# Decay rows of a head stored in one piece in DRAM: one 4096-byte run per partition in the broadcast read

## The chip, the cores and the metric

The kernel runs on one core of one Trainium2 chip. The metric is the device time of one execution in microseconds (us). A core has TensorE (PE), VectorE (DVE), ScalarE (ACT), GpSimd (POOL) and SyncE (SP), which issues nearly all transfers here, and 16 DMA engines that move the data. The engines run apart from one another and meet at semaphores.

## The reference, cut to what matters

One encoder layer in float32, 512 tokens, width 1024. The part that the change touches is a gated delta rule with 8 heads, in both directions of the sequence, in chunks (64 in the reference; the kernel uses 128). Its decay comes from a cumulative sum `gc` over each chunk:

```python
g = -exp(a_log) * softplus(a + dt_bias)          # one number per token, direction and head
gc = cumsum(g, axis=-1)                          # within a chunk
diff = gc[..., :, None] - gc[..., None, :]
decay = where(incl, exp(where(incl, diff, 0.0)), 0.0)
lmat = where(strict, einsum('nbhcd,nbhsd->nbhcs', kb, k) * decay, 0.0)
attn = einsum('nbhcd,nbhsd->nbhcs', q, k) * decay
q_dec = q * exp(gc)[..., None]
```

Around it stand the projections of x by w_in (9216 columns and 32 more), a short convolution branch, two layer norms and a feed-forward part of width 4096.

## The kernel before

Every product of full size is made in three passes over a high and a low part (`xh`, `xl` of the activations, `wh`, `wl` of the weights). A weight block of 128x1024 comes in by one transfer on SP's queue (`raw_in`, 512 KB, line 110, three buffers), ACT makes `wh` from it (line 124), DVE makes `wl` (line 120), and PE runs 24 products of 128x512 (lines 158 to 160, `ps_in`). A load can be issued when DVE has finished with the buffer.

The delta rule is woven into these projections. The code is written as generators, and a loop over slots h = 0..8 sets the order on PE, DVE, ACT and POOL by hand: tables such as `BEGIN` and `MID` say after which step of the projections the next piece of a generator is taken. SP's queue is left to a scheduler. From slot 1 to slot 5 every slot has the same six weight blocks (three of the next head's q, k and v and three of the rest). In each there runs the second half of `gdn_local` of head h (`mid`), the first half of `gdn_local` of head h+1 (`new`) and the scan of head h-1 (`far`).

What the change touches: the cumulative sums of all heads lie in `gc` as 128 tokens by 64 rows (2 directions, 4 chunks, 8 heads). They are transposed to `gct` (64 rows of 128 tokens) and written to `gcd` in DRAM (line 337). For each head, `gdn_local` reads the head's eight rows back to all 128 partitions as `grow` (128 x 8 x 128, 512 KB, line 446, three buffers). DVE makes `dec` from it (line 451), ACT takes the exponential of both (lines 454 and 455), POOL multiplies `grow` with q (line 480), and PE reads the result in the scan (line 660).

What else the prediction speaks of: in the second half of `gdn_local` an inverse of small triangular blocks is made. POOL makes `X` (lines 536 to 550), it goes through DRAM (`xo`, line 555) to `U` (line 559), and PE then runs bursts of very small products: 64 of 32x32 at line 571 (`px`) and 64 at line 580 (`py`), then 32 and 16 at each of the lines 600 and 612 (`pxa`, `pya`, `pxb`, `pyb`). On SP's queue `U`, one `raw_in`, the `grow` of a later head (heads 3 to 7 in the slots 1 to 5) and further `raw_in` follow one another.

Of the kernel before, what the change touches and what calls it, by code (L numbers as in the profile page):

```python
# [8 lines left out]
F32 = mybir.dt.float32  # L9
# [6 lines left out]
P = 128  # L16
# [3 lines left out]
NH = 8  # L20
NCH = 4
# [40 lines left out]
def kernel(  # L62
# [25 lines left out]
    nc = tc.nc  # L88
# [10 lines left out]
    dram = ctx.enter_context(tc.tile_pool(name="dram", bufs=1, space=bass.MemoryType.DRAM))  # L99
# [113 lines left out]
    for d in range(2):  # L213
        t = cons.tile([P, P], F32, name=f"tri{d}")
# [64 lines left out]
    def sm(name, shape=(P, NCH, 16)):  # L279
        return cons.tile(list(shape), F32, name=name)  # L280
# [52 lines left out]
    nc.tensor.transpose(pgt[:64, :P], gcf, ident)  # L333
    gct = sm("gct", (64, P))
    nc.vector.tensor_copy(out=gct, in_=pgt[:64, :P])
    gcd = dram.tile([64, P], F32, name="gcd")
    nc.sync.dma_start(out=gcd, in_=gct)
    urgent.close()
    gcd_v = gcd.rearrange("(d c h) t -> h (d c) t", d=2, c=NCH)


    eye = cons.tile([P, 8, 16], F32, name="eye")
    for g in range(2):
        for t in range(2):
            nc.sync.dma_start(out=eye.rearrange("(b g) (s t) j -> g t b s j", g=2, t=2)[g, t],
                              in_=diag[2 * t + g, 0:4, 0:16].partition_broadcast(P // 2))
# [96 lines left out]
    def gdn_local(h):  # L443

        grow = gdn.tile([P, 2 * NCH, P], F32, tag="grow", name=f"grow{h}", bufs=3)
        nc.sync.dma_start(out=grow, in_=gcd_v[h].partition_broadcast(P))
        yield
        dec = gnear.tile([P, 2 * NCH, P], F32, tag="dec", name=f"dec{h}", bufs=1)
        for c in range(NCH):
# [31 lines left out]
            out=qd, in0=qd,  # L481
            in1=qk[:, 1, :].rearrange("p (c t) -> p c t", t=P).unsqueeze(1).broadcast_to([P, 2, NCH, P]), op=ALU.mult)
        na_ = gdn.tile([P, 2, 2, NCH, P], F32, tag="na", name=f"na{h}", bufs=2)
        for g2 in range(2):
            yield
            pg = ps("g", f"pg{h}_{g2}")
            for cc in range(2):
                c = 2 * g2 + cc
# [25 lines left out]
        for g in range(2):  # L514
            nc.sync.dma_start(out=Nb.rearrange("(b g) i j -> g b (i j)", g=2)[g],
                              in_=xd.rearrange("x a i j -> (x a) (i j)"))
# [21 lines left out]
        t = tmp[:, :7 * 16].rearrange("p (m j) -> p m j", j=16)  # L538
# [3 lines left out]
        for k in range(0, 16, 2):  # L542
# [3 lines left out]
            t = tmp[:, :r * 2 * n].rearrange("p (i m j) -> p i m j", m=2, j=n)  # L546
# [5 lines left out]
        for s_ in range(2):  # L552
            for g in range(2):
                o = slice(16 * s_, 16 * s_ + 16)
                nc.sync.dma_start(out=xo[:, :, o, o].rearrange("x a (r g) j -> g (x a) r j", g=2)[g],
                                  in_=X.rearrange("(b s g) r j -> s g b r j", s=2, g=2)[s_, g])
# [190 lines left out]
    def local(h):  # L747
        state[h] = yield from gdn_local(h)
# [67 lines left out]
    for c in range(8):  # L816
# [11 lines left out]
        t = slab.tile([P, NT], F32, tag="C", name=f"yb{c}", bufs=8)  # L828
        act(out=t, in_=pyb, func=AF.Copy)
        yb.append(t)  # L830
    for c in range(8):
        pgb = proj(w_in[B_GB + c], xh, xl, f"in{B_GB + c}")
        t = slab.tile([P, NT], F32, tag="zt", name=f"sgb{c}", bufs=2)
# [9 lines left out]
    for c in range(8):  # L843
        pga = proj(w_in[B_GA + c], xh, xl, f"in{B_GA + c}")
        t = slab.tile([P, NT], F32, tag="D", name=f"sga{c}", bufs=8)
# [222 lines left out]
```

## Time and profile before

| what | value |
|---|---|
| three runs | 1066.55, 1070.11 and 1071.96 us, median 1070.11 us |
| the profiled execution | 1075.07 us, its span 1073.4 us (from the first to the last instruction) |
| mean granted TensorE clock in it | 0.984 |
| PE busy | 1031.4 us, 96% of the span |
| DVE, ACT, POOL busy | 529.7, 452.6 and 286.6 us |
| moved by DMA | 101.79 MB in 64269 packets |

The profiled execution is 4.96 us above the median. Products on PE are pipelined and their ends are modelled, so busy time is not a measure of work; an idle gap on PE is. The granted clock is 1.00 at 2.4 GHz and 0.50 at 1.2 GHz.

### The profile page before, as it was taken

What the parts mean: (1) busy time and instruction counts of PE and PEld (TensorE: products, weight loads), DVE (VectorE), ACT (ScalarE), POOL (GpSimd) and SP (SyncE); (2) the same over time, 40 slices, a digit from 0 to 9 for tenths busy, and PEclk for the clock granted to TensorE, in tenths of its full rate; (3) what the DMA queues carried; (4) which work ended last, traced back from release to release, by engine and by line L of the source; (5) the groups of instructions that cost most, each with busy time, mean ns of one, the idle gap of its engine ahead of it and who ended that gap; (6) DMA issues with size and microseconds to landing.
All of it is one profiled execution on the core that took longest, in us unless ns stands there. A gap on an engine that the chain in (4) does not pass through costs nothing.

```text
span 1073.4 us, 16601 instructions
## 1 busy us (share of the span) xinstructions
PE 1031.4 (96%) x6611; PEld 854.3 (80%) x6611; DVE 529.7 (49%) x923; ACT 452.6 (42%) x820; POOL 286.6 (27%) x527
## 2 busy tenths in 40 slices
PE   8897989997999999999999999989999999999996
PEld 5676878886878887888888888879888888888885
DVE  6574657665766767352322255581222233333346
ACT  5562546664656575463424233222333343222231
POOL 1061524351535253430131011063222220000005
PEclk9998989998999999999999999999999999999998
DMA  5412242323242513222336324322333343333312
GB/s 197 138 47 88 67 105 67 88 67 87 67 87 67 107 49 92 69 79 79 99 99 233 96 85 138 115 78 63 96 98 98 98 133 102 98 98 94 102 41 79
DMA packets 64269, 101.79 MB, mean 95 GB/s; under 512 B 30720, under 2 KB 40640, under 8 KB 64192
## 3 DMA queue, kind: packets, MB, share of 16 engines
q1 hardware_dynamic: 63760, 100.07, 32.5%
q8 instruction: 52, 0.85, 0.3%
q10 hardware_dynamic: 432, 0.66, 0.2%
q14 instruction: 25, 0.20, 0.1%
HBM read 97.27 MB, written 3.44 MB: 94 GB/s over the span
## 4 chain that ended last, share of the span: by engine, by line
PE 83%; DVE 6%; DMA 3%; POOL 3%; issue 2%; ACT 1%; SPq 1%; POOLq 0%; DVEq 0%; ACTq 0%
PE accd L899 16%; PE ps_in L158 11%; PE ps_in L160 10%; PE ps_in L159 10%; PE ps_up L158 5%; PE ps_up L159 5%; PE ps_up L160 5%; PE acco L899 3%; POOL X L550 2%; PE psup L946 1%; PE ps_osc L158 1%; PE ps_osc L160 1%; PE ps_ogd L158 1%; PE ps_ogd L160 1%; PE ps_osc L159 1%
## 5 line engine op out<-in xcount | busy, mean ns | idle before, releaser
L158 PE MATMUL ps_in<-xh,wh_in 128*128 128x512 f32 x576 | 241.2, 419 | 1.2 <-ACT wh_in L124 1.1
L160 PE MATMUL ps_in<-xh,wl_in 128*128 128x512 f32 x576 | 228.6, 397 | 1.8 <-DVE wl_in L120 1.8
L159 PE MATMUL ps_in<-xl,wh_in 128*128 128x512 f32 x576 | 227.9, 396 | 0.0
L120 DVE TENSOR_TENSOR wl_in<-raw_in,wh_in 128x1024 fp32r<-128x1024 f32 x70 | 95.1, 1358 | 87.1 <-ACT wh_in L124 82.2
L160 PEld LDWEIGHTS ps_in<-xh,wl_in 128*128 128x128 f32 x576 | 109.8, 191 | 27.6 <-DVE wl_in L120 3.0
L158 PEld LDWEIGHTS ps_in<-xh,wh_in 128*128 128x128 f32 x576 | 110.5, 192 | 22.7 <-ACT wh_in L124 2.0
L159 PEld LDWEIGHTS ps_in<-xl,wh_in 128*128 128x128 f32 x576 | 110.8, 192 | 18.3
L124 ACT ACTIVATE wh_in<-raw_in 128x1024 fp32r<-128x1024 f32 x70 | 73.9, 1056 | 71.0 <-PE ps_in L159 52.9
L899 PE MATMUL accd<-wh_down,hh 128*128 128x512 f32 x256 | 99.5, 389 | 0.0
L899 PE MATMUL accd<-wl_down,hh 128*128 128x512 f32 x256 | 99.4, 389 | 0.0
L899 PE MATMUL accd<-wh_down,hl 128*128 128x512 f32 x256 | 99.4, 389 | 0.0
L120 DVE TENSOR_TENSOR wl_up<-raw_up,wh_up 128x1024 fp32r<-128x1024 f32 x30 | 36.8, 1225 | 121.5 <-ACT wh_up L124 121.5
L158 PE MATMUL ps_up<-x1h,wh_up 128*128 128x512 f32 x224 | 87.1, 389 | 0.0
L159 PE MATMUL ps_up<-x1l,wh_up 128*128 128x512 f32 x224 | 87.1, 389 | 0.0
L160 PE MATMUL ps_up<-x1h,wl_up 128*128 128x512 f32 x224 | 87.1, 389 | 0.0
L953 POOL TENSOR_TENSOR hf<-r 128x512 f32<-128x512 f32 x32 | 46.3, 1447 | 118.5 <-ACT r L951 118.5
L124 ACT ACTIVATE wh_up<-raw_up 128x1024 fp32r<-128x1024 f32 x30 | 31.8, 1060 | 106.2 <-PE ps_up L159 98.6
L106 DVE TENSOR_TENSOR wl_down<-raw_down,wh_down 128x1024 fp32r<-128x1024 f32 x32 | 40.1, 1254 | 50.3 <-ACT wh_down L105 48.8
L899 PEld LDWEIGHTS accd<-wh_down,hl 128*128 128x128 f32 x256 | 48.1, 188 | 10.1
L899 PEld LDWEIGHTS accd<-wl_down,hh 128*128 128x128 f32 x256 | 48.1, 188 | 10.0
L899 PEld LDWEIGHTS accd<-wh_down,hh 128*128 128x128 f32 x256 | 48.0, 188 | 10.1 <-ACT wh_down L105 0.4
L105 ACT ACTIVATE wh_down<-raw_down 128x1024 fp32r<-128x1024 f32 x32 | 33.7, 1053 | 51.0 <-PE accd L899 50.3
(268 smaller groups left out, 1853.1 us busy)
## 6 DMA issues: line engine op xcount, KB each, us to landing
raw_in<-in_w_in SPq DMA_DIRECT2D x70, 512.0 KB, 3.7
raw_up<-in_w_up SPq DMA_DIRECT2D x32, 512.0 KB, 3.6
raw_down<-in_w_down SPq DMA_DIRECT2D x32, 512.0 KB, 3.6
grow<-gcd SPq DMA_DIRECT2D x8, 512.0 KB, 10.0
raw_osc<-in_w_o_sc SPq DMA_DIRECT2D x8, 512.0 KB, 3.6
raw_ogd<-in_w_o_gdn SPq DMA_DIRECT2D x8, 512.0 KB, 3.6
raw_out<-in_w_out SPq DMA_DIRECT2D x8, 512.0 KB, 3.7
xr<-in_xT SPq DMA_DIRECT2D x8, 256.0 KB, 5.1
```

What stands on the lines that cost most here:

```text
L105: act(out=hi, in_=src, func=AF.Copy)
L106: (lo_eng or nc.vector).tensor_tensor(out=lo, in0=src, in1=hi.bitcast(F32), op=ALU.subtract)
L120: (nc.gpsimd if pool else nc.vector).tensor_tensor(out=wl, in0=raw, in1=wh.bitcast(F32), op=ALU.subtract)
L124: act(out=wh, in_=raw, func=AF.Copy)
L158: nc.tensor.matmul(acc, wh[:, c], mh[k], start=(k == 0), stop=False)
L159: nc.tensor.matmul(acc, wh[:, c], ml[k], start=False, stop=False)
L160: nc.tensor.matmul(acc, wl[:, c], mh[k], start=False, stop=(k == KT - 1))
L550: sub(out=X[:, 0:r, k + 1:16], in0=X[:, 0:r, k + 1:16], in1=t[:, :, m], op=ALU.add)
L899: nc.tensor.matmul(acc[:, o], a[:, ts_], b[:, hs], start=start and j == 0, stop=stop and j == 2, skip_group_check=True)
L946: nc.tensor.matmul(acc[:, ts_], a[:, c], b[k][:, ts_], start=(k == 0 and t2 == 0 and j == 0), stop=(k == KT - 1 and t2 == 1 and j == 2), s ...
L953: nc.gpsimd.tensor_tensor(out=hfl, in0=r, in1=r, op=ALU.mult)
```

## The change

`gcd` gets one row of 1024 numbers for each head, in the order direction, chunk, token. The write goes through a view of it whose first dimension is the eight pairs of direction and chunk; the read takes one row to all partitions, and the view of `grow` is flat.

```diff
-    gcd = dram.tile([64, P], F32, name="gcd")
-    nc.sync.dma_start(out=gcd, in_=gct)
+    gcd = dram.tile([NH, 2 * NCH * P], F32, name="gcd")
+    nc.sync.dma_start(out=gcd.rearrange("h (x t) -> x h t", t=P), in_=gct)
     urgent.close()
-    gcd_v = gcd.rearrange("(d c h) t -> h (d c) t", d=2, c=NCH)
...
         grow = gdn.tile([P, 2 * NCH, P], F32, tag="grow", name=f"grow{h}", bufs=3)
-        nc.sync.dma_start(out=grow, in_=gcd_v[h].partition_broadcast(P))
+        nc.sync.dma_start(out=grow.rearrange("p x t -> p (x t)"), in_=gcd[h].partition_broadcast(P))
```

On SP, where the write of `gcd` and the reads of the first three heads stand behind the weight loads of head 0:

```order
-L337 DMA gcd<-gct 64x128
-L446 DMA grow_442<-gcd 128x8x128
-L446 DMA grow_581<-gcd 128x8x128
-L446 DMA grow_1206<-gcd 128x8x128
+L338 DMA gcd<-gct 8x8x128
+L446 DMA grow_442<-gcd 128x1024
+L446 DMA grow_581<-gcd 128x1024
+L446 DMA grow_1206<-gcd 128x1024
 L110 DMA raw_in_502<-in_w_in 128x1024
 L110 DMA raw_in_649<-in_w_in 128x1024
```

No transfer has moved: the write has the same 64 rows in another order, and each read has one run in a partition in place of eight. In the later slots the same holds, here the `grow` of head 5 behind `U` of head 3:

```order
 L559 DMA U_2634<-xo_300 128x8x32
 L110 DMA raw_in_2803<-in_w_in 128x1024
-L446 DMA grow_3099<-gcd 128x8x128
+L446 DMA grow_3099<-gcd 128x1024
 L110 DMA raw_in_2921<-in_w_in 128x1024
 L110 DMA raw_in_2976<-in_w_in 128x1024
```

SP has 236 rows before and after, and its places are the same. On PE, where the scan of head 0 first reads `grow`, with the semaphores that a row waits for:

```order
 L656 MATMUL pc_0_1_1275<-S_0_0_1244,y_305 128x128 [waits Activation_49]
 L656 MATMUL pc_1_2_1276<-S_1_3_1247,y_305 128x128 [waits Activation_49]
-L660 MATMUL po_1215<-S_0_0_1244,grow_442 128x128
+L660 MATMUL po_1215<-S_0_0_1244,grow_442 128x128 [waits DMAHW7_49]
 L660 MATMUL po_1215<-S_1_3_1247,grow_442 128x128
 L158 MATMUL ps_in_1209<-xh_80,wh_in_1173 128x512
```

The first product of each head's scan with `grow` has one more wait, for the transfer of that `grow`; POOL's product at line 480 has the same one more for each head. The instructions of PE, DVE, ACT and POOL and their order are the same.

## Rows read from the trace of the kernel before

**Rows 1.** The page: the span, PE's busy time, and a DMA queue (packets, MB, share).

```profile
span 1073.4 us, 16601 instructions
...
PE 1031.4 (96%) x6611; PEld 854.3 (80%) x6611; DVE 529.7 (49%) x923; ACT 452.6 (42%) x820; POOL 286.6 (27%) x527
...
q8 instruction: 52, 0.85, 0.3%
```

**Rows 2.** Transfers of the whole program: count, size, median us from issue to landing.

```profile
raw_in<-in_w_in SPq DMA_DIRECT2D x70, 512.0 KB, 3.7
...
grow<-gcd SPq DMA_DIRECT2D x8, 512.0 KB, 10.0
...
ln_g<-in_ln_g SPq DMA_DIRECT2D x2, 512.0 KB, 3.8
ln_b<-in_ln_b SPq DMA_DIRECT2D x2, 512.0 KB, 6.3
...
gcd<-gct SPq DMA_DIRECT2D x1, 32.0 KB, 1.8
```

**Rows 3.** Stretches between `py` of successive heads: length, busy times, PEclk, DMA.

```profile
148.07:203.29 55.22, 51.85 (x469) 42.91 (x468) 34.95 (x79) 30.58 (x69) 19.49 (x55) 0.94 0.30 73
203.29:252.09 48.80, 48.80 (x469) 40.93 (x468) 34.98 (x79) 30.64 (x69) 20.52 (x55) 1.00 0.34 85
252.09:309.58 57.49, 51.13 (x469) 42.56 (x468) 35.62 (x79) 30.63 (x69) 20.59 (x55) 0.94 0.31 72
309.58:360.02 50.44, 49.02 (x470) 41.02 (x469) 35.62 (x79) 30.65 (x69) 20.34 (x55) 1.00 0.39 81
360.02:409.29 49.27, 48.87 (x469) 40.94 (x468) 34.60 (x79) 30.65 (x69) 20.56 (x55) 1.00 0.34 79
```

**Rows 4.** PE in order of time: start, us, what, [idle before <-releaser].

```profile
155.12 0.26 PE L600 MATMUL pxa<-U,na 32*32 32x32 f32 x1 [2.95 <-issue]
...
252.09 0.72 PE L580 MATMUL py<-U,lx 32*32 32x32 f32 x60
259.18 0.32 PE L580 MATMUL py<-U,lx 32*32 32x32 f32 x4 [6.36 <-issue]
...
315.04 0.18 PE L600 MATMUL pxa<-mt,na 32*32 32x32 f32 x1 [1.42 <-issue]
```

**Rows 5.** Two stretches behind such gaps, columns as in rows 3.

```profile
155.12:161.45 6.33, 6.33 (x46) 4.58 (x46) 0.51 (x4) 1.78 (x9) 2.50 (x13) 0.50 0.06 21
...
259.18:263.85 4.67, 4.67 (x14) 3.65 (x14) 4.21 (x10) 1.24 (x3) 0.00 (x0) 0.50 0.02 7
```

**Rows 6.** Instruction packets that begin in 0.1 us from 152.7, 256.8 and 312.5.

```profile
q8 instruction: 1, 0.02, 60.1%
...
q8 instruction: 1, 0.02, 60.6%
...
q8 instruction: 1, 0.02, 54.9%
```

**Rows 7.** SP in order of time: issues of the transfers before these packets.

```profile
142.28 0.38 SPq L446 DMA_DIRECT2D grow<-gcd  x1
...
246.42 0.53 SPq L110 DMA_DIRECT2D raw_in<-in_w_in  x1
247.04 0.38 SPq L446 DMA_DIRECT2D grow<-gcd  x1
...
304.48 0.38 SPq L446 DMA_DIRECT2D grow<-gcd  x1
```

**Rows 8.** Head 0: SP's issues; landings of tile grow; DVE's first instruction on it.

```profile
33.83 5.11 SPq L446 DMA_DIRECT2D grow<-gcd  x3
...
DMA to landing us min/median/max: 8.2/10.0/16.4
...
42.59 0.60 DVE L451 SCALAR_TENSOR_TENSOR dec<-grow,gc,madd 128x128 f32<-128x128 f32 x2
```

**Rows 9.** Line 446: a wait as an instruction of its own, ns min/median/max.

```profile
L446 SPq EVENT_SEMAPHORE  x6: 17/17/17, 32.6 to 354.8; - x6
```

## The prediction

> **What bounds the kernel now.** I read the page first: PE is busy for 96% of a span of 1073.4 us [rows 1]. The time can only fall by what PE stands still, or by what it runs at a low clock. Next I read the transfers: a `grow` takes 10.0 us from issue to landing, a weight block of the same 512 KB 3.7 us [rows 2]. That is the difference the change is about, so the question is who pays for it.
>
> Directly, nobody does. In the view of waits no engine is ever released by the landing of a `grow`. Head 0 is closest: the first `grow` is issued at 33.83 and lands 8.2 us later, the shortest of all, at 42.0; DVE begins with it at 42.59, without a wait [rows 8]. All later heads have more room. The view of tile `grow` says the same: who waits there waits for ACT.
>
> So I looked for what else a slow transfer can hold up, in the slots that have one. From `py` of one head to `py` of the next PE does the same work five times, 469 or 470 products [rows 3]. It takes 48.80 and 49.27 us in the second and fifth stretch, with PE busy all the time at clock 1.00, but 55.22, 57.49 and 50.44 us in the first, third and fourth. The mean of the clean ones is 49.03, so the others lose 6.19, 8.46 and 1.41 us: **16.06 us in all**.
>
> PE's timeline shows where: gaps of 2.95, 6.36 and 1.42 us, each in the middle of a burst of tiny products, and each put down to "issue", which is the page's word for a wait on nothing it can see [rows 4]. Behind the first two the granted clock is 0.50 for 6.33 and 4.67 us [rows 5]; PE had been idle just before it fell. At half speed half of such a stretch is lost: 2.95 + 3.17 = 6.12 and 6.36 + 2.34 = 8.70, and the third is 1.42 alone. Their sum, 16.24, is the excess of rows 3 within 0.2 us, so nothing else is in it.
>
> What does PE wait for? The q8 queue moves 52 packets of instructions, 0.85 MB, that is some 16 KB each [rows 1]. PE has 2 x 6611 products and weight loads; 0.85 MB over 13222 is 64 bytes for each, so I take q8 to be PE's own program. One such packet begins at 152.7, 256.8 and 312.5 [rows 6], and PE goes on at 155.12, 259.18 and 315.04, 2.4 to 2.5 us later each time [rows 4]. PE had run out of instructions. On the average a packet of some 256 instructions lasts 1073.4 / 52 = 20.6 us; but in a burst 60 tiny products with their weight loads, nearly half a packet, are gone in 0.72 us [rows 4], and then a late packet shows.
>
> And why was it late? A `grow` was issued at 142.28, 247.04 and 304.48 [rows 7]. With 10.0 us each they land at about 152.3, 257.0 and 314.5 [rows 2]. The three packets begin 0.4 after, 0.2 before and 2.0 before these landings. Program and data share the 16 DMA engines, and I read this as the program's packet standing behind the `grow`.
>
> The Trainium skill ("Runtime: NRT & Kernel Launch", Instruction fetch mechanics) says that an engine's program comes in blocks of 16 KiB, 256 instructions, which the rows bear out. It also says that the fetch is mostly hidden; here three gaps of 10.73 us speak against that, and if they had another cause the change would bring nothing, which is the first rival below.
>
> **The change, part by part.**
>
> *The read.* Eight runs of 512 bytes become one of 4096. Before has two transfers of exactly this form, the layer norm's rows broadcast to all partitions, 512 KB in runs of 4096: `ln_g` lands in 3.8 us, `ln_b` in 6.3 us with other transfers around it [rows 2]. I take these as bounds in place of 10.0. Eight transfers times 3.7 to 6.2 us saved are nothing on the path by themselves; what counts is when the program's packet gets through.
>
> To cost nothing, a packet must begin 2.4 us before PE runs dry. PE ran dry at 152.17, 252.82 and 313.62 (resumption less gap, rows 4), so the latest starts are 149.8, 250.4 and 311.2. Changed, the `grow` lands at 146.1 to 148.6 in the first stretch and at 308.3 to 310.8 in the fourth: both packets are in time, the one by 0.8 us or more with its lag of 0.4, the other by 0.4 or more. In the third it lands at 250.8 to 253.3, because PE reaches its burst sooner after the issue; with the packet 0.2 before that, it is 0.2 to 2.7 us late. A weight load issued 0.62 us before it is still in flight [rows 7], so I take the middle, a landing after 5.0 us and a gap of 1.4. The gap of 1.42 us in the fourth stretch was followed by no slow clock (that stretch shows 1.00, rows 3), so I add none. At the far end a gap of 2.7 is like that of 2.95, which cost 3.17 more: 5.9 stay.
>
> *The write of `gcd`.* Same 64 rows, other places. It is not shown in its new form; it lands in 1.8 us now [rows 2]. If it took three times as long, 3.6 us more, the first `grow` would be issued at 37.4 and land by 43.7 even at 6.3 us, 1.1 us after DVE wants it; at 3.8 us it lands at 41.2, in time. I take nothing, and 1.1 us, once, as the upper bound.
>
> *Issue on SP.* The first three reads keep SP for 5.11 us [rows 8]. The weight load behind them waits for DVE to leave its buffer anyhow (in the view of SP's waits that is its longest kind), so a shorter issue gains nothing. The weight loads that follow a `grow` will land earlier, but no split of a weight block waits for a landing there now, so this is nothing too; the three buffers cover it, and without them every such load would show its time to landing.
>
> *The added waits.* Sixteen, eight on PE and eight on POOL, all for transfers that landed long before. A wait as an instruction of its own took 17 ns [rows 9]: at most 0.27 us. Behind PE's wait stands the rest of its program, but it never has to hold.
>
> *What is late next.* With the gaps gone PE would be fed by the next thing in line. The clean stretches say what that is: PE busy 48.80 of 48.80 us with the same DVE, ACT and POOL work [rows 3]. Nothing else stands close. The later stages wait for PE, so what is gained stays.
>
> Sum: 6.19 + (8.46 - 1.4) + 1.41 - 0.27 = **14.4 us**; bounds 16.06 - 0.2 = 15.9 and 16.06 - 5.9 - 0.27 - 1.1 = 8.8. The profiled execution would go from 1075.07 to 1060.7 (span 1059.0).
>
> The runs shown are another matter: their median, 1070.11, is 4.96 us below the profiled execution. If the same gaps are in them, the median falls to 1055.7. If the 4.96 us are gaps that they do not have, the gain is 9.4 and the median 1060.7. I take **1058**, between the two.
>
> **The rivals.**
>
> *No change (1070).* Either the program's packets are late by themselves, or unprofiled executions lack the gaps. For it: nobody waits for a `grow`, and in the second and fifth stretch a `grow` of the same kind costs nothing. Against it: all three gaps fall at the end of a `grow`, and none elsewhere in the slots. It would also come about if the transfer were no faster. The Trainium skill ("DMA: Bandwidth & Descriptors", Specifications) puts the least transfer for full rate at 512 bytes, which the old runs already have. The trace disagrees, with 10.0 us for these and 3.7 to 6.3 for runs of 4096 [rows 2]; by the rule the time would stay at 1070.
>
> *Half of it (1060 to 1067).* The packet gets stuck behind the weight loads in place of the `grow`. If the first and the third stretch both keep a gap like that of 2.7 us with a slow clock behind it, 2 x 5.9 stay and 16.06 - 11.8 - 0.3 = 4.0 us are gained: 1066. For it: 4096-byte weight loads stand in the queue too. Against it: they land in 3.7 us.
>
> *Slower (up to 1100).* All 128 partitions now read the same 4096 bytes in the same order at the same time. If that made a `grow` slower than 10.0 us, the five stretches would get a longer gap or a new one; at 16.4 us, the longest of today [rows 8], 6.4 us in each of five stretches, 32 us in all: 1102. The point from which it decides is a landing of more than 10 us. `ln_g` with its 3.8 us speaks against it.
>
> **How the numbers follow.** The forecast gets 0.67, half of it 0.13, no change 0.16, slower 0.04. A difference of 0.5% (5.35 us; the three runs differ by 5.41) is about what these runs can tell. Faster than 1064.8 takes the forecast and 0.09 of the half: 0.76. Same takes no change and the rest of the half: 0.20. Slower 0.04. The range begins at the fastest run less 15.9, 1051, and goes to 1067, the end of the second rival; what lies outside is no change and slower, 0.20.
>
> **What would show it.** Right: `grow` to landing at 4 to 6 us; no "issue" gap on PE above 2 us in the slots; the first, third and fourth stretch at 49 to 51 us with clock 1.00; each instruction packet of the slots begins earlier after the issue of its `grow`. Wrong: a `grow` at 8 us or more; gaps at the same places although `grow` lands early, which would make the fetch late for another cause; or gaps gone and the time the same, which would mean that another engine takes over.

## The result, and the profile after

The changed kernel takes 1057.62 us, the median of 4 runs (1056.44 to 1058.42). Before took 1070.36 us on the same chip, the median of 4 (1066.55 to 1071.96). The ratio is 0.9885, with a 95% interval of 0.9857 to 0.9913: 12.7 us less, where the forecast was 1058.0 and 12.1 less.

The page of the changed kernel, the lines that answer to [rows 1, 2]:

```profile
span 1054.7 us, 16601 instructions
...
PE 1025.2 (97%) x6611; PEld 850.6 (81%) x6611; DVE 532.5 (50%) x923; ACT 452.6 (43%) x820; POOL 286.2 (27%) x527
...
q8 instruction: 52, 0.85, 0.3%
...
grow<-gcd SPq DMA_DIRECT2D x8, 512.0 KB, 4.8
```

A `grow` now lands in 4.8 us in place of 10.0. The same instructions and the same 52 packets of program are there; the span is 18.7 us shorter, and PE's busy time has fallen by 6.2 us with the same number of products, because fewer of them ran at the low clock.

The stretches from `py` to `py` in the changed kernel, columns as in [rows 3]:

```profile
145.06:194.20 49.14, 48.88 (x470) 40.93 (x469) 34.95 (x79) 30.59 (x69) 20.51 (x55) 1.00 0.28 75
194.20:243.00 48.80, 48.80 (x470) 40.92 (x469) 35.07 (x79) 30.64 (x69) 20.34 (x55) 1.00 0.31 85
243.00:292.42 49.42, 49.01 (x470) 41.02 (x469) 35.62 (x79) 30.65 (x69) 20.53 (x55) 1.00 0.31 84
292.42:341.23 48.81, 48.81 (x469) 40.92 (x468) 35.64 (x79) 30.65 (x69) 20.52 (x55) 1.00 0.30 85
341.23:390.29 49.06, 48.88 (x469) 40.94 (x468) 34.99 (x79) 30.65 (x69) 20.62 (x55) 1.00 0.26 73
```

All five are now what only the second and fifth were: 48.8 to 49.4 us at clock 1.00. Their sum is 245.23 us; before it was 261.22. So 15.99 of the 18.7 us that the span lost come from here. 3.01 us come from ahead of them, since the first stretch begins at 145.06 in place of 148.07, and 0.30 are given back behind them.

PE in order of time, the waits of over 0.2 us that are left in the five stretches and at their end (columns as in [rows 4]):

```profile
244.13 0.25 PE L580 MATMUL py<-U,lx 32*32 32x32 f32 x4 [0.41 <-issue]
...
391.17 0.31 PE L580 MATMUL py<-U,lx 32*32 32x32 f32 x10 [0.21 <-issue]
```

SP in order of time, the issues of the first three `grow` and of those that stand before the three packets of [rows 6]:

```profile
33.78 1.28 SPq L446 DMA_DIRECT2D grow<-gcd  x3
...
139.27 0.33 SPq L446 DMA_DIRECT2D grow<-gcd  x1
...
237.96 0.38 SPq L446 DMA_DIRECT2D grow<-gcd  x1
...
287.31 0.38 SPq L446 DMA_DIRECT2D grow<-gcd  x1
```

The queues of the changed kernel, packets that begin in 0.1 us from 145.5, 241.9 and 291.3:

```profile
q8 instruction: 1, 0.02, 60.1%
...
q8 instruction: 1, 0.02, 60.0%
...
q8 instruction: 1, 0.02, 54.9%
```

The reader should subtract: a packet of PE's program begins 6.2, 3.9 and 4.0 us after the issue of the `grow` ahead of it. Before it was 10.4, 9.8 and 8.0 [rows 6, 7]. Of these three only the middle one still comes late, by 0.41 us. The gap of 0.21 at 391.17 is not owed to a `grow`: the last of them was issued at 336.06 and landed 5.0 us later. So a burst can run ahead of its program by a little with no slow read in flight.

### The profile page after: what moved, and what is told of

Its sections match the earlier page's. It is cut to its first block, busy times and chain, and to the rows that moved or that the text cites. A ratio compares the mean times of both kernels' runs of the same rounds, so it can differ in the third digit from the quotient of the medians.

```text
span 1054.7 us, 16601 instructions
## 1 busy us (share of the span) xinstructions
PE 1025.2 (97%) x6611; PEld 850.6 (81%) x6611; DVE 532.5 (50%) x923; ACT 452.6 (43%) x820; POOL 286.2 (27%) x527
## 4 chain that ended last, share of the span: by engine, by line
PE 84%; DVE 6%; DMA 3%; POOL 3%; ACT 1%; issue 1%; SPq 1%; POOLq 0%; DVEq 0%; ACTq 0%
PE accd L899 16%; PE ps_in L158 11%; PE ps_in L160 10%; PE ps_in L159 10%; PE ps_up L159 5%; PE ps_up L160 5%; PE ps_up L158 5%; PE acco L899 3%; POOL X L550 2%; PE psup L946 1%; PE ps_osc L158 1%; PE ps_osc L160 1%; PE ps_osc L159 1%; PE ps_ogd L159 1%; PE ps_ogd L160 1%; PE ps_ogd L158 1%
## 5 line engine op out<-in xcount | busy, mean ns | idle before, releaser
L158 PE MATMUL ps_in<-xh,wh_in 128*128 128x512 f32 x576 | 238.5, 414 | 1.2 <-ACT wh_in L124 1.0
L160 PE MATMUL ps_in<-xh,wl_in 128*128 128x512 f32 x576 | 226.2, 393 | 1.8 <-DVE wl_in L120 1.8
L120 DVE TENSOR_TENSOR wl_in<-raw_in,wh_in 128x1024 fp32r<-128x1024 f32 x70 | 97.4, 1391 | 86.9 <-ACT wh_in L124 86.3
L899 PEld LDWEIGHTS accd<-wh_down,hh 128*128 128x128 f32 x256 | 48.0, 188 | 10.4 <-ACT wh_down L105 0.4
L899 PEld LDWEIGHTS accd<-wh_down,hl 128*128 128x128 f32 x256 | 48.0, 188 | 10.1
```

Source lines behind the costliest of these rows:

```text
L120: (nc.gpsimd if pool else nc.vector).tensor_tensor(out=wl, in0=raw, in1=wh.bitcast(F32), op=ALU.subtract)
L158: nc.tensor.matmul(acc, wh[:, c], mh[k], start=(k == 0), stop=False)
L160: nc.tensor.matmul(acc, wl[:, c], mh[k], start=False, stop=(k == KT - 1))
L899: nc.tensor.matmul(acc[:, o], a[:, ts_], b[:, hs], start=start and j == 0, stop=stop and j == 2, skip_group_check=True)
```

## The experiments

Each ran beside the kernel before on the same chip, and a median of before named below was measured beside the run. Landings are median us from issue to landing of the eight `grow`. A gap is a wait of PE put down to "issue"; gaps behind the fifth stretch, up to 0.73 us, are left out.

**The kernel before, once more.** No edit.

> The kernel before, unchanged, profiled a second time. Theory (PE's program packets stand behind the grow transfers): idle gaps of PE put down to issue again in the stretches from py to py of heads 1 to 5, at the same instructions (the 61st product of py in the third stretch, within pxa in the first and the fourth), together 4 to 16 us with the slow clock behind them; grow to landing 10 us; time 1066 to 1075. Rival (the gaps belonged to that one execution): gaps at other places or none, and the stretches all at 49 us.

It took 1073.06 us; before has a median of 1072.37 (13 runs). PE in order of time:

```profile
94.88 0.22 PE L600 MATMUL pxa<-U,na 32*32 32x32 f32 x3 [1.80 <-issue]
...
153.90 0.21 PE L600 MATMUL pxa<-U,na 32*32 32x32 f32 x1 [2.83 <-issue]
...
257.35 0.32 PE L580 MATMUL py<-U,lx 32*32 32x32 f32 x4 [6.75 <-issue]
...
312.95 0.18 PE L600 MATMUL pxa<-mt,na 32*32 32x32 f32 x1 [1.87 <-issue]
```

The three gaps of [rows 4] come back at the same products, with nearly the same lengths, and one more in slot 0. They belong to the program and are not an accident of one execution; so the runs that are only timed should have them too, which one rival doubted.

**The program shifted by 64 instructions.** Unused products at the very start, in the kernel before.

```diff
         nc.tensor.matmul(warm[:, :P], ones, ones, start=True, stop=True)
+    for i in range(16):
+        nc.tensor.matmul(warm[:32, :32], ones[:32, :32], ones[:32, :32], start=True, stop=True)
```

> The kernel before with 16 more products of 32x32 on PE at its very start (results unused): as rows of PE they are 32 products and 32 weight loads, so all that follows lies 64 instructions later in PE's program, a quarter of a packet, while every transfer, grow with its 512-byte runs too, stays as it was. Theory (program packets behind grow): each packet is now asked for some 7 us earlier against the work, which in the five slots is before the grow is issued; the gaps of 2.95, 6.36 and 1.42 us vanish or move to other places; grow still lands after 10 us; the five stretches come to 49 to 51 us and the time to 1055 to 1062. Rival (the landing of grow itself, or its traffic, slows the kernel): the time stays at 1066 to 1072, with the same gaps.

1070.75 us (10 runs), ratio 0.998 (0.9958 to 1.0002); `grow` 10.0. The time that I had expected did not come, but the gaps moved. PE in order of time:

```profile
153.20 0.40 PE L160 MATMUL ps_in<-xh,wl_in 128*128 128x512 f32 x1 [2.22 <-issue]
...
258.04 0.40 PE L158 MATMUL ps_in<-xh,wh_in 128*128 128x512 f32 x1 [0.62 <-issue]
...
304.97 0.79 PE L160 MATMUL ps_in<-xh,wl_in 128*128 128x512 f32 x1 [4.17 <-issue]
...
359.67 0.50 PE L159 MATMUL ps_in<-xl,wh_in 128*128 128x512 f32 x1 [1.75 <-issue]
```

They now stand before ordinary products of the projection, which need nothing that is late. Why there? Count PE's products and weight loads from the start to each gap. First the kernel before, to its three gaps (columns as in [rows 3]; the counts are in brackets behind PE and PEld), then the shifted one, to its four:

```profile
0.00:154.90 154.90, 135.74 (x982) 108.16 (x982) 98.62 (x213) 80.35 (x146) 42.97 (x100) 0.96 0.38 110
0.00:259.00 259.00, 233.02 (x1871) 189.46 (x1872) 163.49 (x355) 140.37 (x279) 82.97 (x210) 0.96 0.35 96
0.00:314.80 314.80, 287.46 (x2379) 234.51 (x2380) 203.38 (x444) 172.26 (x350) 103.56 (x265) 0.96 0.35 92
```

```profile
0.00:152.90 152.90, 134.81 (x982) 108.34 (x983) 97.77 (x211) 80.33 (x146) 42.80 (x100) 0.96 0.38 109
0.00:257.90 257.90, 239.03 (x1998) 194.84 (x1999) 170.44 (x376) 143.99 (x294) 84.25 (x218) 0.97 0.36 99
0.00:304.80 304.80, 281.79 (x2380) 230.91 (x2380) 204.63 (x447) 172.25 (x350) 103.34 (x265) 0.97 0.35 96
0.00:359.50 359.50, 334.74 (x2888) 274.51 (x2888) 240.34 (x525) 204.67 (x427) 123.68 (x320) 0.97 0.35 93
```

Before: 1964, 3743, 4759. Shifted: 1965, 3997, 4760, 5776. The differences, 1779, 1016, 2032, 763 and 1016, are 7, 4, 8, 3 and 4 times 254, within 1. PE runs dry only where one packet's worth of its program ends (16 KB at 64 bytes are 256; two in each would then be rows that are neither product nor load), whatever instruction stands there. Why no time was gained was argued and not tried: I had counted on 64 instructions to bring the request forward by some 7 us. But in a burst 60 products with their loads take 0.72 us [rows 4], so the packet was probably asked for hardly earlier; the four gaps still sum to 8.76 us, against 10.73 before.

**The same short runs, closer together.** Eight runs of 512 bytes, 528 apart, in place of 4096 apart.

```diff
+    gcd = dram.tile([NH, 2 * NCH, P + 4], F32, name="gcd")
+    nc.sync.dma_start(out=gcd.rearrange("h x t -> x h t")[:, :, :P], in_=gct)
...
+        nc.sync.dma_start(out=grow, in_=gcd[h][:, :P].partition_broadcast(P))
```

> The changed layout with a gap of 16 bytes behind each row of 128: a head's eight rows lie one behind the other in DRAM as in the change, but the read is still eight runs of 512 bytes in a partition. Theory (the length of a run sets the landing): grow lands after 9 to 11 us and the time is that of before, 1066 to 1073. Rival (what helps is that a head's rows are neighbours): grow lands after 4 to 6 us and the time is 1056 to 1060.

1059.79 us (4 runs), ratio 0.9867 (0.9843 to 0.9891); one gap, 0.96 us, in the third stretch. Its `grow`:

```profile
DMA to landing us min/median/max: 4.1/5.4/7.3
```

My theory that the short run is what makes the old read slow fell here: 512 bytes at a time land in nearly half of the old time.

**Two runs of 2048 bytes, 16 KB apart.** One row for each direction of a head, two writes.

```diff
+    gcd = dram.tile([2, NH, NCH * P], F32, name="gcd")
+    for d in range(2):
+        nc.sync.dma_start(out=gcd[d].rearrange("h (c t) -> c h t", t=P), in_=gct[32 * d:32 * d + 32])
...
+        nc.sync.dma_start(out=grow.rearrange("p (d c) t -> p d (c t)", d=2), in_=gcd[:, h, :].partition_broadcast(P))
```

> One size between the two kernels: two runs of 2048 bytes (one for each direction) in place of eight of 512 or one of 4096; the write of gcd becomes two. Theory (a transfer of 512 KB has a cost per run): with 10.0 us for 1024 runs and 4.8 us for 128, 5.8 us per 1000 runs, grow lands after 5 to 6 us; the program packets come in time; time 1056 to 1061. Rival (only the single run helps, or 4096 bytes is a step): landing near 10 us, time 1066 to 1072.

1061.74 us (4 runs), ratio 0.9874 (0.9841 to 0.9908); `grow` 6.4; one gap of 1.81 us with a low clock behind it, so that the third stretch takes 52.39 us. Landing and time are a little above what I had expected. Runs four times as long as those of the last experiment were not faster. What was left as a cause was how far apart the runs lie.

For the next three runs I made a reckoning, with the times of the changed kernel for PE. It takes a packet to be asked for when PE is 150 rows into a block of 256, and to be held until 9.8 us after the issue of a slow `grow`. The 150 is an assumption that no view here shows. The reckoning says for any shift of the program which blocks come late and by how much.

**The kernel before, program 200 instructions later.** Fifty tiny unused products in slot 0.

```diff
+                if h == 0 and u == 20:
+                    pad_ps = ps("l", "pad_ps")
+                    for i in range(50):
+                        nc.tensor.matmul(pad_ps[:32, :32], ones[:32, :32], ones[:32, :32], start=True, stop=True)
                 step(own if own and u < 3 * KT else fill)
```

> The kernel before with 50 unused products of 32x32 in one piece on PE in slot 0 (100 products and 100 weight loads as PE's rows): all behind them lies 200 instructions later in PE's program; transfers and the order of all else are as before, grow with its slow reads too. Theory (a program packet asked for while a grow is in flight waits for its end; PE runs dry at every 256th instruction that comes before the packet): laid over the after trace's times, with packets held until 9.8 us after a grow's issue, 200 leaves one gap of 2.8 us in five stretches where 0 leaves 12; time 1058 to 1064 with the 1.2 us that the products take. Rival (the slow grow costs the time in another way): 1068 to 1076.

1064.62 us (4 runs), ratio 0.9921 (0.9893 to 0.9949), with `grow` at 10.2 as slow as ever. PE's waits from 100 to 430 us (us in total, times, longest):

```profile
PE pxa L600 <- issue: 2.6, 1, 2.6
PE px L571 <- DVE UT L564: 1.0, 2, 0.6
PE pya L612 <- issue: 0.3, 1, 0.3
```

One gap of 2.6 us is left, and one of 0.3: work was added, the read left alone, and the kernel became faster by 7.4 us.

**The kernel before, 88 instructions later.** The same edit with 22 products.

> The same with 22 products, 88 instructions later. By the same reckoning this is nearly the worst place: gaps of about 5.8, 3.8, 6.6 and 3.2 us in four of the five stretches, 19 us, and slow clock behind some; time 1074 to 1086. Rival (the place in the program doesn't matter): as the run with 50 products, less 0.7 us.

1077.46 us (10 runs), ratio 1.0043 (1.0027 to 1.0059). PE in order of time:

```profile
153.09 0.21 PE L580 MATMUL py<-U,lx 32*32 32x32 f32 x1 [5.24 <-issue]
...
210.23 0.32 PE L600 MATMUL pxa<-U,na 32*32 32x32 f32 x5 [2.39 <-issue]
...
312.19 0.33 PE L580 MATMUL py<-U,lx 32*32 32x32 f32 x7 [4.72 <-issue]
...
368.71 0.22 PE L600 MATMUL pxa<-U,na 32*32 32x32 f32 x2 [2.72 <-issue]
```

Four gaps in four of the five stretches, as reckoned, each shorter than the reckoning gave. The third stretch, without a gap, takes 48.81 us, the others 56.65, 54.20, 55.19 and 53.32. Counted as above, the gaps are at 1965, 2981, 4760 and 5776, again multiples of 254 apart, within 1. Before this shift the second and the fifth stretch were the clean ones [rows 3]; now both have a gap. A clean stretch is luck of the place.

**The changed kernel, 88 instructions later.** The same 22 products behind the new read.

> The changed kernel with the same 22 products at the same place. Theory: a grow that lands after 4.8 us holds a packet for no more than that; by the reckoning gaps of 0.6 and 1.4 us, time 1057 to 1062, some 20 us less than the kernel before at the same shift. Rival (the gain of the change is a lucky place in the program): the gaps of 3 to 7 us come back, time 1068 or more.

1056.43 us (4 runs), ratio 0.9851 (0.9825 to 0.9876); `grow` 4.6; stretches 48.81, 48.82, 48.81, 49.79 and 48.82, the fourth with a gap of 0.80. The edit that costs the slow kernel 5.5 us (1077.46 against a median of 1071.98) costs the changed one nothing that can be seen, and the time is half a microsecond below what I had expected. Whether it helps can't be said: the interval overlaps that of the plain change.

**The changed kernel with the old read beside it, unused.** A second `gcd` in the old order, read into DRAM with each `grow`.

```diff
+        jk = dram.tile([P, 2 * NCH, P], F32, tag="jk", name=f"jk{h}", bufs=8)
+        nc.sync.dma_start(out=jk, in_=gcs_v[h].partition_broadcast(P))
```

> The changed kernel, which behind each grow also makes the old read (eight rows of 512 bytes that lie 4096 bytes apart, to 128 places) from a second copy of the sums into a DRAM tile that nobody uses. Theory (any slow transfer in the queue holds the packets): grow itself lands after 4 to 7 us, and still PE runs dry again at its 256th instructions, 5 us or more in all; time 1064 to 1085. Rival (it needs grow's own landing): no gaps over 1 us, time 1056 to 1061.

1070.47 us (one run). This one went astray: with nobody waiting for them, all eight unused reads were issued at the beginning, and none in the later slots. The five stretches have no gap (48.79 to 49.41 us). The first `py` starts at 103.59, 15.1 us later than in the changed kernel; PE ahead of it in order of time:

```profile
82.79 0.80 PE L158 MATMUL ps_in<-xh,wh_in 128*128 128x512 f32 x1 [4.17 <-ACT wh_in L124]
...
102.02 1.08 PE L576 MATMUL px<-UT,dg 32*32 32x32 f32 x64 [11.32 <-DVE UT L569]
```

That is ordinary waiting for other engines in a crowded start. The time is by chance that of before, and says nothing on the question asked. One packet of program does fall among the unused reads, which land after 14.9 us here (median), the last at 80.3 us: it begins at 65.67, when PE has come to row 489, where the changed kernel's begins at 59.5 and row 422. So it seems that a read can delay a packet though nobody waits for it, but one packet in a crowded start doesn't show it, and the packet did not wait for the last of these reads.

The last four experiments were made to settle what makes the old read slow. Before has a median of 1074.0 (7 runs) beside them.

**Rows of a head 4224 bytes apart.** The kernel before with 16 bytes behind each row of `gcd`; same order, same write, same eight runs of 512.

```diff
-    gcd = dram.tile([64, P], F32, name="gcd")
+    gcd = dram.tile([64, P + 4], F32, name="gcd")[:, :P]
```

> The kernel before with 16 bytes behind each row of 128 in DRAM and nothing else: a head's eight rows of 512 bytes lie 4224 bytes apart in place of 4096. Theory A (a pitch of 4096 puts all eight rows behind one another at the same place of the memory): grow lands after 5 to 6 us, time 1057 to 1062. Theory B (eight rows far apart are slow whatever the pitch): grow lands after 9 to 11 us, time 1068 to 1076.

1061.73 us (4 runs), ratio 0.9884 (0.9868 to 0.99). Its `grow`, the gap that is left, and the stretch with that gap, from three views (tile, PE in order of time, stretches):

```profile
DMA to landing us min/median/max: 5.9/6.4/11.3
```

```profile
248.34 0.25 PE L580 MATMUL py<-U,lx 32*32 32x32 f32 x4 [2.67 <-issue]
```

```profile
244.94:298.23 53.29, 50.62 (x469) 42.22 (x469) 35.64 (x79) 30.62 (x69) 20.29 (x55) 0.97 0.32 79
```

Sixteen bytes that nobody reads give 12.3 us. The third stretch keeps 4.5 us more than a clean one: 2.67 of gap, and the rest from the clock behind it, 0.97 in the mean.

**Rows 2048 bytes apart.** As in the experiment with rows 528 apart, with `4 * P` in place of `P + 4`.

> Eight rows of 512 bytes of a head 2048 bytes apart. Theory A: a power of two again, landing between 5.4 (528 apart) and 10 us (4096 apart), some 7 to 9 us. Theory B: the same, by the distance. It is the third point of a row 528, 2048, 4096, 8192.

1060.80 us (one run); one gap, 1.66 us, third stretch 50.67. Its `grow`:

```profile
DMA to landing us min/median/max: 5.4/6.0/12.2
```

Both theories had put it higher. A power of two is not enough to make it slow.

**Rows 8192 bytes apart.** The kernel before with each row of `gcd` twice as long.

```diff
-    gcd = dram.tile([64, P], F32, name="gcd")
+    gcd = dram.tile([64, 2 * P], F32, name="gcd")[:, :P]
```

> The kernel before with rows twice as far apart: a head's eight rows of 512 bytes lie 8192 bytes apart. Theory A (power-of-two pitch): landing 10 us or more, up to 16 us if half as many places are used again; PE's gaps longer, time 1070 to 1085. Theory B (distance): 10 us or a little more.

1118.4 us (one run), span 1116.7. Its `grow`, and PE's waits from 100 to 430 us:

```profile
DMA to landing us min/median/max: 14.2/17.0/33.3
```

```profile
PE pxa L600 <- issue: 17.5, 2, 8.8
PE py L580 <- issue: 12.7, 1, 12.7
PE pya L612 <- issue: 11.6, 2, 5.8
```

Five gaps in five stretches, 41.8 us in all, from nothing but a slower `grow`. With the order, the instructions and the bytes unchanged, this is the mechanism in its plainest form. Not all of the time is of this kind: the first `py` starts at 97.61, 6.1 us later than in the profile of before, and here DVE does wait for the first `grow`, 5.46 us, which no engine did at 10 us.

**The changed kernel, once more.** No edit.

> The changed kernel, unchanged, on the same chip as the padded kernel. Theory: grow lands after 4.8 us, no issue gap of PE over 1 us in the five stretches; time 1055 to 1060, and within 3 us of the padded kernel if theory A holds.

1059.52 us (4 runs), ratio 0.9866 (0.9849 to 0.9882); `grow` 5.0; gap 0.26; stretches 49.18, 48.79, 49.28 and 48.81. Against the 4224 bytes of pitch measured beside it the medians differ by 2.2 us and the intervals overlap; the profiled third stretch is 4.0 us shorter.

## Why the prediction was right, and where it was not

**What PE waited for: right.** It was read from three coincidences. The runs showed it three ways: the gaps stay at the same count of PE's rows when other instructions stand there; moving the program by 88 or 200 instructions moves the time to 1077 or 1065 us with the same slow read; and a `grow` of 17 us brings five gaps. The queues show the packet tied to the `grow`. Us from the issue of `grow` to its own landing, and to the begin of the packet that follows, in the five stretches (the trace has no landing for one):

| kernel | landing of `grow` | begin of the packet |
|---|---|---|
| changed | 3.6, -, 4.7, 4.8, 5.0 | 6.2, 4.5, 3.9, 4.0, 4.8 |
| before | 9.6, 9.8, 10.3, 9.7, 10.1 | 10.4, 9.3, 9.8, 8.0, 9.7 |
| rows 8192 apart | 15.4, 16.0, 17.0, 17.5, 17.0 | 16.2, 15.5, 16.1, 15.6, 16.0 |

Where the read is slow the packet begins within 2 us of the landing, in the clean stretches of before too. Their `grow` and packets, from SP in order of time and from the queues (packets that begin in 0.1 us from 207.9 and 364.5):

```profile
198.63 0.38 SPq L446 DMA_DIRECT2D grow<-gcd  x1
...
354.84 0.38 SPq L446 DMA_DIRECT2D grow<-gcd  x1
```

```profile
q8 instruction: 1, 0.02, 58.4%
...
q8 instruction: 1, 0.02, 71.0%
```

Counted as above, PE comes to the ends of these blocks, rows 2981 and 5775, at 210.5 and 367.1, some 2.5 us after the packets begin, which is just enough. This answers what the first rival had for it, that a `grow` costs nothing in the second and fifth stretch: the packet is held there as long and is needed later. By what the `grow` holds the packet, the DMA engines that both share or something else, was not tried apart, since the one run meant for it went astray.

The Trainium skill ("Runtime: NRT & Kernel Launch", Instruction fetch mechanics) gives an engine's program store as only two blocks of 16 KiB, filled in sequence; the same section also names 128 KiB for PE, which would be eight. The counts above agree with blocks of that size, and the trace of before with two of them: between the packets at 130.84 and 152.74 PE goes from row 1433 to row 1964, about two blocks, and stands still. Its rule that the fetch is mostly hidden holds in the changed kernel (0.41 us) and not in the one before.

**The clock: right.** The low clock behind the first and third gap is gone with them; the granted clock of all five stretches is 1.00. In the other runs it fell behind gaps of 1.81 us and more in these stretches, though not behind each (not behind the 2.6 us of the program 200 later nor the 1.87 us of the repeat of before, whose stretches show 1.00), and behind none that was shorter.

**The sum: right in its main term.** Forecast for the first, third and fourth stretch were 6.19, 7.06 and 1.41 us; they gave 6.08, 8.07 and 1.63, and the fifth 0.21. The third is larger because the gap left there was taken as 1.4 and is 0.41: its packet begins 3.9 us after the issue of `grow`, where 4.8 had been taken.

**Not in the sum: 3.0 us ahead of the stretches.** All of it lies before the first `py`, at 88.46 in place of 91.49. Two things differ there. The clock from 42.0 to 45.4 is 1.00, where before it was 0.50; and PE waits 3.13 us for `UT` ahead of `px`, where before it waited 5.14. The first does not follow the read: the low clock came again with rows 2048 apart and with the changed read in the run of 88 instructions, and did not with rows 528 or 4224 apart. The second was 3.12 in the other profile of the changed kernel, 4.88 to 5.21 with rows 528, 2048 and 4224 apart and with two runs, but 1.24 in the repeat of before. What sets it stays open. So the profiled pair fell by 18.63 us where 14.4 was forecast.

**The median: right, and by luck so close.** The profiled execution of before was 4.71 us above the median of the runs. I had put the median between 1055.7 and 1060.7; it is 1057.62, and 1059.52 in the repeat. The repeat of before, 1073.06 beside a median of 1072.37, has the same gaps, so they are not what made that first profile slow; what did stays open. That 1058 lies within 0.4 us of the result is luck: it is the middle of two readings, neither of which knew of the 3 us ahead of the stretches, and the profiled pair fell by 18.6 us where the medians fell by 12.7.

**Costs taken as nothing: right.** The write of `gcd` delays the first `grow` little: SP issues it 1.97 us after the write, before 1.85. The first `grow` is issued at 33.78, and DVE begins with it at 42.41, at 42.59 before. Even the longest landing of all, 5.9 us, would be at 39.7. PE's products at line 660 show no wait, and of POOL's seven separate waits at line 480 six take 43 ns, before 17. The first of them, at 38.00, takes 6.63 us, far more than the 17 ns in the prediction; it waits for DVE's `dec` as well as for the landing, and costs nothing, since POOL's product then waits for ACT up to 50.52.

**Why the old read was slow: wrong.** "*The read.* Eight runs of 512 bytes become one of 4096", and then the price from two transfers with runs of 4096: the prediction put the 10.0 us down to the length of a run. The runs by distance, with the landings: runs of 512 bytes 528 apart 5.4 us, 2048 apart 6.0, 4224 apart 6.4, 4096 apart 10.0, 8192 apart 17.0; one run 4.8 and 5.0. It is the distance of 4096 and of 8192 bytes that costs, and 4224 does not. The price was right since one run has no such distance; the length by itself is worth at most some 0.4 to 1.6 us. Two runs 16 KB apart took 6.4, so a large distance between only two runs does not do it.

The Trainium skill ("DMA: Bandwidth & Descriptors", Latency and other measured facts) tells of slow copies where the pitch of rows in HBM is a large power of two, from 2 MiB up, and of a pad that restores the rate. The runs here agree in kind but show it at 4 and 8 KiB, and a pad of 128 bytes in the pitch was enough, where the page found 192 bytes too few. The rule of 512 bytes that was weighed in the first rival is thus not refuted by the old read: runs of 512 land in 5.4 to 6.4 us where their distance is another.

**The rivals.** *No change* needed gaps of another cause; they went with the slow read. *Half of it* did not come with the changed read. The gap with a slow clock behind it that it priced at 5.9 us is seen in the kernel with rows 4224 apart, where the third stretch keeps 4.5, but behind a `grow` that lands after 6.4 us and not behind weight loads. *Slower* is refuted: 128 readers of the same 4096 bytes land in 4.8 us.

## What to carry to other kernels

Before a broadcast or strided read is called hidden because nobody waits for its landing, look for "issue" gaps of the busiest engine and for the instruction queue's packets just before they end: a slow transfer can hold up the program itself, and the bill comes at whatever instruction stands at the end of a block. Where several rows that are read together lie 4 or 8 KB apart, as the eight here, try to pad them or to put them behind one another first; 2 KB, and 16 KB between two rows, were not slow. And where a kernel's time moves by 1% on an edit that adds a few instructions, count the instructions to its gaps before the edit is praised or blamed.

## What the runs showed that I had not expected

- Place in the program is worth 13 us with the slow read: 88 more instructions give 1077.46 us, 200 more 1064.62. With the fast read 88 more cost nothing.
- The distance of rows sets the landing of the same 512 KB from 5.4 to 17.0 us, and with it the time from 1059.79 to 1118.4. The three first issues on SP go with it: 1.28 us for one run, 2.00, 2.94 and 3.43 for rows 528, 2048 and 4224 apart, 5.11 for 4096, 7.25 for 8192. What in the memory or the queues does that was not tried.
- From the begin of a late packet to PE's next product it takes 2.2 us in the changed kernel (241.9 to 244.13), 2.4 to 2.5 before.
